# MLP up products on TensorE: moving columns read, and PSUM columns written, in another order

## The chip, the cores and the metric

The kernel runs on one core of a Trainium2 chip. A core has TensorE (PE in the profile; PEld is its weight load), VectorE (DVE), ScalarE (ACT), GpSimd (POOL) and SyncE (SP, which here mostly issues transfers). The metric is the device time of one execution in microseconds (us); lower is better.

## The reference

A two-layer decoder trunk on 1024 positions of width 1024, all in float32. Layer 0 mixes tokens by a gated DeltaNet, layer 1 by sliding-window attention. The part that matters here is the gated MLP, which each layer has once:

```python
D_FF = 2816

def causal_dwconv(x, w):
    k_w = w.shape[0]
    t = x.shape[1]
    xp = jnp.pad(x, ((0, 0), (k_w - 1, 0), (0, 0)))
    y = w[0] * xp[:, 0:t]
    for i in range(1, k_w):
        y = y + w[i] * xp[:, i:i + t]
    return y

def conv_ffn(x, w_up, conv_w, w_down):
    u = causal_dwconv(x @ w_up, conv_w)
    gate, val = u[..., :D_FF], u[..., D_FF:]
    return (jax.nn.silu(gate) * val) @ w_down

def reference(...):
    h = x
    for i in range(DEPTH):
        ...
        h = h + conv_ffn(rmsnorm(h, norm_ffn[i]), f_w_up[i], f_conv[i], f_w_down[i])
        ...
    return rmsnorm(h, norm_final)
```

The change touches how `x @ w_up` is computed, and not what it gives.

## The kernel before

Activations lie transposed: 128 channels on the partitions, 1024 positions along the free dimension, eight such tiles for the width of 1024. A matmul takes a 128 x 128 block of weights as its stationary operand and streams 512 columns (positions) of activations through it into one PSUM bank of 512 columns. To keep float32 accuracy with the faster float32r type, each operand is split into a high and a low part, and a product is made of three passes: high by high, high weights by low activations, low weights by high activations.

The MLP is the function `ffn`. For each of 22 values of j (`NF`) it computes a 128-row tile of the gate and one of the value. The two tiles, the two halves of the positions and the even and odd input tiles make a 2 x 2 by 2 x 2 block product, and it is done with seven products instead of eight (Winograd's form of Strassen's scheme). `Mix.add` makes the seven activation operands: `b11`, `b21`, `b22` are plain blocks, `t1` to `t4` are sums and differences of blocks. In the profile `b11` is in the tile named b (high part in columns 0 to 511, low part in 512 to 1023), `t1` and `t2` share the tiles t12h and t12l (one half each), `t3` and `t4` share t34h and t34l, and `b21` and `b22` share x1h and x1l. `weights` loads and adds up the weight blocks and splits them into `whi` and `wlo`.

`prod` runs one product: over four input tiles k, three matmuls each, so 12 matmuls into one PSUM bank. `up` runs the seven for one j, in the order b11, t2, t3, t1, b21, t4, b22. p1 takes b11 and later b21, p7 takes t3 and later t4, p5 takes t1 and later b22, p6 takes t2 alone. p6 is in the pool whose banks the profile names d, the others in the one named mm. Between them VectorE and ScalarE take the sums out of PSUM, and `step` runs pieces of the down product (gh and gl by dhi and dlo in the profile), 12 matmuls each, into banks named d.

What sets the order: SyncE, VectorE, ScalarE, GpSimd and TensorE each run their own queue in the order in which the program was written, as far as the tile framework keeps it. `E.pinned = True` keeps TensorE's matmuls in program order through `ffn`'s loop. All matmuls are issued from one helper, so the profile puts them on line 152, and groups are told apart by their tiles.

The prediction also uses rows from elsewhere: line 654, GpSimd's triangular solve in layer 0, where the pass j works on rows of j + 1 elements in a 16 x 16 table (15 - j rows of them, 16 apart); line 736, where ScalarE copies four blocks of 64 columns out of PSUM to places 128 apart; and lines 778 and 1347, ScalarE's copies out of PSUM without a break.

Of the kernel before, what the change touches and what calls it, by code (L numbers as in the profile page):

```python
# [90 lines left out]

def ch(t, c):
    return t[:, c * P:(c + 1) * P]


def hs(h):
# [12 lines left out]
def kernel(  # L109
# [104 lines left out]
    def passes(ps, wh, wl, xs, h, k0=0):  # L214

        n = len(xs)
        for k, (xh, xl) in enumerate(xs):
            w_h, w_l = ch(wh, k0 + k), ch(wl, k0 + k)
            E.matmul(ps, w_h, xh[:, hs(h)], start=k == 0, stop=False)
            yield  # L220
            E.matmul(ps, w_h, xl[:, hs(h)], start=False, stop=False)
            yield
            E.matmul(ps, w_l, xh[:, hs(h)], start=False, stop=k == n - 1)
            yield

    def mm3(ps, wh, wl, xs, h, k0=0, first=True, last=True):
        n = len(xs)
        for k, (xh, xl) in enumerate(xs):
            w_h, w_l = ch(wh, k0 + k), ch(wl, k0 + k)
            E.matmul(ps, w_h, xh[:, hs(h)], start=first and k == 0, stop=False)  # L230
            E.matmul(ps, w_h, xl[:, hs(h)], start=False, stop=False)
            E.matmul(ps, w_l, xh[:, hs(h)], start=False, stop=last and k == n - 1)
# [26 lines left out]
    class Norm:  # L259
# [23 lines left out]
        def factor(self):  # L283
            ps = pst()
            for c in range(NCH):
                E.matmul(ps[:, c:c + 1], ch(self.sq, c), ones[:, 0:1], start=True, stop=True)
            S.put(self.sq)
            ms = sm.tile([P, NCH], F32, tag="ms", name="ms")
            V.tensor_scalar(ms, ps[:, 0:NCH], 1.0 / D, EPS, MUL, ADD)
            r = sm.tile([P, NCH], F32, tag="r", name="r")  # L290
            G.tensor_tensor(r, ms, mhalf, ALU.pow)
            self.r = r
# [916 lines left out]
    def ffn(l, mix, nxt):  # L1209
# [60 lines left out]

        def prod(ps, w, xn, ks=range(KT // 2), first=True):
            wh, wl = w
            for k in ks:
                xh, xl = mix.x[xn][k]
                mm = dict(skip_group_check=not first)
                E.matmul(ps, ch(wh, k), xh, start=first and k == 0, stop=False, **mm)
                E.matmul(ps, ch(wh, k), xl, start=False, stop=False, **mm)
                E.matmul(ps, ch(wl, k), xh, start=False, stop=k == KT // 2 - 1, **mm)
# [52 lines left out]
        def up(j, early, late):  # L1331
# [12 lines left out]
            else:  # L1344
                p1 = pmt()
                prod(p1, *take(), "b11")
                A.copy(dd, p1)
                for _ in range(early[0]):
                    step()
                p6 = pdt()  # L1350
                prod(p6, *take(), "t2")
                V.tensor_tensor(dd, p6, dd, SUB)
                if j == 1:
# [8 lines left out]
                gated(j - 1)  # L1362
                p7 = pmt()
                prod(p7, *take(), "t3")
                V.tensor_tensor(zh(z2, 1), p7, dd, ADD)  # L1365
                p5 = pmt()
# [81 lines left out]
        for j in range(NF):  # L1448
            n = len(todo) + len(loaded)
# [234 lines left out]
```

## Time and profile before

| | |
|---|---|
| median of 2 runs | 2771.84 us |
| lowest and highest run | 2769.29 and 2774.39 us |
| profiled execution, its own time | 2775.09 us |
| its span, first to last instruction | 2773.3 us |
| mean granted TensorE clock | 0.985 |
| MLP up products, layer 0 | 742 to 1398 us of the span |
| MLP up products, layer 1 | 1930 to 2588 us of the span |
| HBM traffic | 232.56 MB read, 99.68 MB written |

The page of the profile comes from one execution. Busy time of an engine is the union of its instructions, so overlapping matmuls count once. In a row of a group, the number after the x is the count, then come the busy time in us and the mean duration in ns of one, then the idle time of the engine just before them. In a row of the timeline the two numbers ahead are start and duration in us.

### The profile page before, as it was taken

Reading aid. Unit: us, or ns where it says so; the run is one execution under the profiler, and the core shown is the slowest. Engines: PE = TensorE matmul, PEld = TensorE weight load, DVE = VectorE, ACT = ScalarE, POOL = GpSimd, SP = SyncE. Lnnn points to the kernel's source line nnn. Section 1 sums busy time; section 2 is a strip of 40 time slices with the busy share of each in tenths; the row PEclk is TensorE's granted clock in tenths of the full one; section 3 lists DMA queues with packets and bytes.
Section 4 is the critical chain, followed back from the end, with each engine's and each line's share of the span. In section 5 each row is a group of like instructions: output and inputs, shape, how many; then the busy total and the mean of one; then the engine's idle time right before and its main releaser. Section 6 shows DMA issues by size and latency. Waiting matters only on the chain. (4 is left out here: it accounts for less than half of the span.)

```text
span 2773.3 us, 35355 instructions
## 1 busy us (share of the span) xinstructions
PE 2664.3 (96%) x12914; PEld 2141.2 (77%) x12914; DVE 1790.9 (65%) x2579; ACT 1119.6 (40%) x2184; POOL 1175.5 (42%) x1104
## 2 busy tenths in 40 slices
PE   9899999999899999999999999999999999999998
PEld 7778878878677787787777776667777888888786
DVE  6555555564787777677764336656867767677745
ACT  5443334442633333333343235555433333333443
POOL 5444444342454444445432323334544444444354
PEclk9999999999999999999999999999999999999999
DMA  5222221232225555555432221222255555554323
GB/s 175 88 72 57 64 59 55 64 101 70 103 87 184 184 175 196 197 192 182 162 106 72 82 69 46 56 68 100 86 173 181 185 188 176 201 196 154 108 91 109
DMA packets 167069, 340.83 MB, mean 123 GB/s; under 512 B 38896, under 2 KB 91504, under 8 KB 166896
## 3 DMA queue, kind: packets, MB, share of 16 engines
q1 hardware_dynamic: 166032, 337.20, 36.9%
q8 instruction: 101, 1.65, 0.3%
q10 hardware_dynamic: 864, 1.38, 0.1%
q14 instruction: 72, 0.59, 0.1%
HBM read 232.56 MB, written 99.68 MB: 120 GB/s over the span
## 5 line engine op out<-in xcount | busy, mean ns | idle before, releaser
L201 POOL TENSOR_TENSOR wlo<-wraw,whi 128x512 fp32r<-128x512 f32 (+1 forms) x204 | 273.6, 1358 | 407.4 <-ACT whi L198 365.0
L152 PE MATMUL mm<-xh,whi 128*128 128x512 f32 x856 | 358.2, 418 | 3.6 <-ACT xh L254 2.7
L152 PE MATMUL mm<-xh,wlo 128*128 128x512 f32 x856 | 349.7, 409 | 0.0
L152 PE MATMUL mm<-xl,whi 128*128 128x512 f32 x856 | 347.1, 406 | 0.5 <-DVE xl L255 0.5
L211 POOL TENSOR_TENSOR dlo<-draw,dhi 128x256 fp32r<-128x256 f32 (+1 forms) x160 | 164.9, 1031 | 350.5 <-ACT dhi L210 329.2
L1226 POOL TENSOR_TENSOR wlo<-wraw,whi 128x512 fp32r<-128x512 f32 x132 | 188.9, 1439 | 155.4 <-ACT whi L1225 155.4
L1226 POOL TENSOR_TENSOR wlo<-sa,whi 128x512 fp32r<-128x512 f32 x132 | 194.1, 1471 | 139.2 <-ACT whi L1225 139.2
L152 PE MATMUL d<-gh,dhi 128*128 128x512 f32 x576 | 229.7, 399 | 6.4 <-DVE h L1325 6.0
L152 PE MATMUL d<-gh,dlo 128*128 128x512 f32 x576 | 228.3, 396 | 0.0
L152 PE MATMUL d<-gl,dhi 128*128 128x512 f32 x576 | 228.2, 396 | 0.0
L1325 DVE TENSOR_TENSOR h<-h,d 128x512 f32<-128x512 f32 x288 | 193.8, 682 | 32.9 <-PE d L152 32.4
L198 ACT CAST whi<-wraw 128x1024 fp32r<-128x1024 f32 (+3 forms) x122 | 100.1, 822 | 234.2 <-PE mm L152 114.2
L152 PEld LDWEIGHTS mm<-xh,wlo 128*128 128x128 f32 x856 | 163.4, 191 | 34.0
L152 PEld LDWEIGHTS mm<-xh,whi 128*128 128x128 f32 x856 | 163.9, 191 | 31.1 <-ACT xh L254 3.1
L152 PEld LDWEIGHTS mm<-xl,whi 128*128 128x128 f32 x856 | 164.3, 192 | 27.5 <-DVE xl L255 1.3
L152 PE MATMUL mm<-t34h,whi 128*128 128x512 f32 x352 | 141.4, 402 | 5.8 <-DVE zv L1365 4.7
L321 DVE SCALAR_TENSOR_TENSOR yf<-zg,fcv,yf 128x1024 f32<-128x1024 f32 x88 | 131.0, 1489 | 18.3 <-ACT yf L319 16.7
L152 PE MATMUL mm<-t34l,whi 128*128 128x512 f32 x352 | 140.9, 400 | 0.8 <-POOL t34l L914 0.8
L152 PE MATMUL mm<-t34h,wlo 128*128 128x512 f32 x352 | 140.7, 400 | 0.0
L152 PE MATMUL mm<-x1l,whi 128*128 128x512 f32 x352 | 139.4, 396 | 0.2
L152 PE MATMUL mm<-x1h,whi 128*128 128x512 f32 x352 | 139.4, 396 | 0.0
L152 PE MATMUL mm<-x1h,wlo 128*128 128x512 f32 x352 | 139.2, 396 | 0.0
(376 smaller groups left out, 6559.6 us busy)
## 6 DMA issues: line engine op xcount, KB each, us to landing
hf<-h SPq DMA_DIRECT2D x160, 512.0 KB, 3.3
h<-hf SPq DMA_DIRECT2D x160, 512.0 KB, 4.2
wraw<-f_up SPq DMA_DIRECT2D x88, 512.0 KB, 3.4
draw<-f_down SPq DMA_DIRECT2D x144, 128.0 KB, 2.3
wraw<-a_in SPq DMA_DIRECT2D x32, 512.0 KB, 3.6
wraw<-g_w SPq DMA_DIRECT2D x24, 512.0 KB, 3.3
row<-rowd SPq DMA_DIRECT2D x16, 512.0 KB, 3.9
wraw<-b_in SPq DMA_DIRECT2D x12, 512.0 KB, 3.6
```

The lines of the kernel that those rows point to most:

```text
L152: i = nc.tensor.matmul(*a, **k)
L198: A.copy(hi, raw)
L201: G.tensor_tensor(lo[:, i:j], raw[:, i:j], hi[:, i:j].bitcast(F32), SUB)
L211: G.tensor_tensor(lo, raw, hi[:, :].bitcast(F32), SUB)
L321: V.scalar_tensor_tensor(dst[:, a:b], z[:, a + i:b + i], w[:, i:i + 1], dst[:, a:b], MUL, ADD)
L1226: G.tensor_tensor(lo, src, hi.bitcast(F32), SUB)
L1325: V.tensor_tensor(t[:, hs(h)], t[:, hs(h)], ps, ADD)
```

## The change

`prod` passes its PSUM bank and its moving operands through a function of the product's name before the matmuls are issued. The function views columns 0 to 511 as m parts of equal length and takes n columns from each part in turn. With `runs(2, 2)`, t2 reads columns 0, 1, then 256, 257, then 2, 3, then 258, 259, and so on, and writes its results to the same columns of the bank. So each result lands where it did before; only the order in time within a matmul differs. The stationary operands keep theirs. With `runs(256, 2)` the order is that of before, and `b11` passes through as it is.

```diff
+def runs(n, m):
+
+    return lambda ap: ap[:, 0:512].rearrange("p (m r n) -> p r m n", m=m, n=n)
+
+
+ORDERS = {
+    "b11": lambda ap: ap,
+    "t2": runs(2, 2),
+    "t3": runs(8, 2),
+    "t1": runs(16, 2),
+    "b21": runs(32, 2),
+    "t4": runs(16, 4),
+    "b22": runs(256, 2),
+}
...
         def prod(ps, w, xn, ks=range(KT // 2), first=True):
             wh, wl = w
+            order = ORDERS[xn]
+            ps = order(ps)
             for k in ks:
-                xh, xl = mix.x[xn][k]
+                xh, xl = (order(v) for v in mix.x[xn][k])
                 mm = dict(skip_group_check=not first)
                 E.matmul(ps, ch(wh, k), xh, start=first and k == 0, stop=False, **mm)
```

Every engine has the same instructions in the same order, with the same waits. On TensorE the shape of five products' matmuls differs (partitions first, then the sizes of the nested loops over the columns); the helper's line moves from 152 to 168. TensorE before, at the end of t2 and the start of the down product's matmuls, at one j in layer 0:

```order
L152 MATMUL d_10987<-t12h_225_6195,whi_10819 128x512
L152 MATMUL d_10987<-t12l_226_6196,whi_10819 128x512
L152 MATMUL d_10987<-t12h_225_6195,wlo_10820 128x512
L152 MATMUL d_10987<-t12h_235_6298,whi_10819 128x512
L152 MATMUL d_10987<-t12l_236_6299,whi_10819 128x512
L152 MATMUL d_10987<-t12h_235_6298,wlo_10820 128x512
L152 MATMUL d_11003<-gh_369_10309,dhi_10964 128x512
```

TensorE after the change, at the same place:

```order
L168 MATMUL d_10987<-t12h_225_6195,whi_10819 128x128x2x2
L168 MATMUL d_10987<-t12l_226_6196,whi_10819 128x128x2x2
L168 MATMUL d_10987<-t12h_225_6195,wlo_10820 128x128x2x2
L168 MATMUL d_10987<-t12h_235_6298,whi_10819 128x128x2x2
L168 MATMUL d_10987<-t12l_236_6299,whi_10819 128x128x2x2
L168 MATMUL d_10987<-t12h_235_6298,wlo_10820 128x128x2x2
L168 MATMUL d_11003<-gh_369_10309,dhi_10964 128x512
```

The rows stand where they stood; t2's 512 columns are now 128 rounds of two parts with two columns each, and the down product's matmul is unchanged.

TensorE before, at the same j, from the end of t1 to the start of b21:

```order
L152 MATMUL mm_11051<-t12h_235_6298,whi_10856 128x512
L152 MATMUL mm_11051<-t12l_236_6299,whi_10856 128x512
L152 MATMUL mm_11051<-t12h_235_6298,wlo_10857 128x512
L152 MATMUL mm_10944<-x1h_207_6051,whi_10945 128x512
L152 MATMUL mm_10944<-x1l_208_6052,whi_10945 128x512
L152 MATMUL mm_10944<-x1h_207_6051,wlo_10946 128x512
```

TensorE after the change, at the same place:

```order
L168 MATMUL mm_11051<-t12h_235_6298,whi_10856 128x16x2x16
L168 MATMUL mm_11051<-t12l_236_6299,whi_10856 128x16x2x16
L168 MATMUL mm_11051<-t12h_235_6298,wlo_10857 128x16x2x16
L168 MATMUL mm_10944<-x1h_207_6051,whi_10945 128x8x2x32
L168 MATMUL mm_10944<-x1l_208_6052,whi_10945 128x8x2x32
L168 MATMUL mm_10944<-x1h_207_6051,wlo_10946 128x8x2x32
```

Nothing moved here either; t1 has 16 rounds of two parts with 16 columns each, b21 has 8 rounds of two parts with 32 columns each.

## The prediction

> **What bounds the kernel now.** I read the page first: its line of busy times and, among the forty slices, the row of the granted TensorE clock.
>
> ```profile
> span 2773.3 us, 35355 instructions
> PE 2664.3 (96%) x12914; PEld 2141.2 (77%) x12914; DVE 1790.9 (65%) x2579; ACT 1119.6 (40%) x2184; POOL 1175.5 (42%) x1104
> PEclk9999999999999999999999999999999999999999
> ```
>
> TensorE (PE) is busy for 96% of the span, with the clock nearly always open, and the next engine, VectorE (DVE), for 65%. Since 96% is an average, I then asked for the two stretches that hold the MLP up products, one per layer (columns: length, busy time of each engine, granted clock, DMA share, GB/s):
>
> ```profile
> core 0: us, PE busy (x) PEld busy (x) DVE busy (x) ACT busy (x) POOL busy (x), PEclk, DMA share, GB/s
> 742.00:1398.00 656.00, 649.60 (x2775) 519.20 (x2774) 483.92 (x575) 243.40 (x378) 306.15 (x231) 1.00 0.51 174
> 1930.00:2588.00 658.00, 649.75 (x2772) 519.65 (x2771) 481.30 (x574) 243.53 (x376) 298.00 (x228) 0.99 0.50 170
> ```
>
> PE stands idle for 656.00 - 649.60 = 6.4 us in the first and 658.00 - 649.75 = 8.25 us in the second. What it waits for in the second is listed by the view of waits (total us, times, longest):
>
> ```profile
> PE d L152 <- DVE h L1325: 4.1, 3, 1.8
> PE mm L152 <- DVE zv L1365: 2.3, 1, 2.3
> PE mm L152 <- DVE t12l L914: 0.7, 1, 0.7
> ```
>
> So no engine covers PE there. Time added to the up products' matmuls comes out at the end nearly one for one: at most 6.4 + 8.25 = 14.65 us of idle time could swallow some. Time taken off them would be gained until VectorE, at 483.92 of 656 us, is the bound, which is far away.
>
> A matmul's own duration (396 ns and more in the groups below) overlaps its neighbours; what counts is the step from one start to the next. It is read from the timeline of PE, here at one value of j where the products stand in a row; each of these rows is the first of a product's twelve matmuls (start us, duration us):
>
> ```profile
> 1017.82 0.40 PE L152 MATMUL d<-t12h,whi 128*128 128x512 f32 x1
> ...
> 1020.62 0.40 PE L152 MATMUL d<-gh,dhi 128*128 128x512 f32 x1
> ...
> 1023.45 0.40 PE L152 MATMUL mm<-t34h,whi 128*128 128x512 f32 x1
> ...
> 1026.25 0.40 PE L152 MATMUL mm<-t12h,whi 128*128 128x512 f32 x1
> ...
> 1029.05 0.40 PE L152 MATMUL mm<-x1h,whi 128*128 128x512 f32 x1
> ...
> 1031.85 0.40 PE L152 MATMUL mm<-t34h,whi 128*128 128x512 f32 x1
> ...
> 1034.65 0.40 PE L152 MATMUL d<-gh,dhi 128*128 128x512 f32 x1
> ```
>
> t2 runs from 1017.82 to 1020.62, then t3, t1, b21 and t4 each start 2.80 us after the one before, and t4 ends at 1034.65. Each of the five takes 2.80 us, that is 2.80 / 12 = 0.2333 us a matmul, whichever tile it reads and whichever PSUM bank it writes.
>
> **The change, part by part.** It adds and removes no instruction on any engine and moves none; every wait stays on the instruction that had it. What differs is the order in which a matmul walks its 512 moving columns, and with them its 512 PSUM columns. How many matmuls that touches follows from the groups (the page's, all of one form; count after the x):
>
> ```profile
> L152 PE MATMUL mm<-t34h,whi 128*128 128x512 f32 x352 | 141.4, 402 | 5.8 <-DVE zv L1365 4.7 <-DVE zv L1342 1.2
> L152 PE MATMUL mm<-x1h,whi 128*128 128x512 f32 x352 | 139.4, 396 | 0.0
> L152 PE MATMUL mm<-b,whi 128*128 128x512 f32 x352 | 110.8, 396 | 0.0
> L152 PE MATMUL d<-t12h,whi 128*128 128x512 f32 x176 | 69.6, 396 | 0.0
> L152 PE MATMUL mm<-t12h,whi 128*128 128x512 f32 x176 | 69.6, 396 | 0.0
> ```
>
> Each tile pair has three such groups (high by high, low by high, high by low). t34 serves t3 and t4: 3 x 352 = 1056, so 528 each. t12 serves t2 (into d) and t1 (into mm): 3 x 176 = 528 each. x1 serves b21 and b22, 528 each. b11 keeps its order by the table, and b22's two runs of 256, one behind the other, are again columns 0 to 511 in order. So the last two are unchanged, and five products, 5 x 528 = 2640 matmuls, walk in pieces. In one matmul of t2 there are 512 / 2 = 256 pieces, of t3 64, of t1 32, of b21 16 and of t4 32, together 400.
>
> The sum is 2640 matmuls times an unknown extra per matmul. No matmul of this kernel walks in pieces, so the extra is bounded by the nearest rows. The first is what the stream of columns is limited by now. In layer 1 there is a stretch in which the granted clock is half (window row, then timeline):
>
> ```profile
> 2025.80:2029.20 3.40, 3.40 (x10) 2.62 (x9) 1.79 (x3) 0.44 (x2) 1.03 (x1) 0.50 0.38 154
> ```
>
> ```profile
> 2027.83 0.63 PE L152 MATMUL mm<-t34h,whi 128*128 128x512 f32 x1
> 2028.26 0.63 PE L152 MATMUL mm<-t34l,whi 128*128 128x512 f32 x1
> 2028.69 0.63 PE L152 MATMUL mm<-t34h,wlo 128*128 128x512 f32 x1
> ```
>
> There the step is (2028.69 - 2027.83) / 2 = 0.43 us. Half of it is 0.215, and at the full clock the step is 0.2333: about 0.018 us of each step isn't the array's clock. Matmuls of 256 columns show the same pace, from 1663.91 to 1664.38 in four steps, 0.1175 each, or 0.46 ns a column, like 0.2333 / 512:
>
> ```profile
> 1663.91 0.28 PE L152 MATMUL d<-kh,qa 128*128 128x256 f32 x1
> ...
> 1664.38 0.40 PE L152 MATMUL mm<-xh,whi 128*128 128x512 f32 x1
> ```
>
> So something that goes with the columns, perhaps the way they are read or written, is slightly slower than the array. That is why I don't call a cost impossible. From below, 0.215 us is the pace of the array: the change can gain at most 0.018 x 2640 = 48 us. From above, the one slower pace in these rows is 0.43: 0.197 x 2640 = 520 us.
>
> The second set of rows is how other engines fare with broken patterns. POOL's line 654 works on a 16 x 16 table, at 544.42 (its second pass) on 14 rows of 2 and at 481.46 (its last but one) on 2 rows of 14, both 28 elements, and both reading and writing the table in place. ACT's line 736 writes 256 elements as four runs of 64, and 128 and 512 elements without a break stand beside it:
>
> ```profile
> 544.42 0.24 POOL L654 TENSOR_TENSOR sys<-sys 64x28 f32<-64x28 f32 x1
> ```
>
> ```profile
> 481.46 0.23 POOL L654 TENSOR_TENSOR sys<-sys 64x28 f32<-64x28 f32 x1
> ```
>
> ```profile
> L778 ACT COPY u<-s 128x128 f32<-128x128 f32 x64 | 16.9, 264 | 55.8 <-PE s L152 55.5
> L1347 ACT COPY sb<-mm 128x512 f32<-128x512 f32 x42 | 24.4, 582 | 46.5 <-PE mm L152 46.5
> L736 ACT COPY X<-d 64x256 f32<-64x256 f32 x16 | 5.9, 367 | 31.8 <-PE d L156 31.8
> ```
>
> On POOL twelve more pieces, each of two 4-byte elements as in t2, cost 0.01 us or nothing (the rows are rounded to that). On ACT the straight line between 264 and 582 ns gives 264 + 128 x 318 / 384 = 370 ns for 256 elements, and the broken write took 367. An access pattern with pieces is free there. I take the extra as 0 for all five products, since these are the only rows of broken patterns and the shortest piece among them is also two elements; both ends stay for the range.
>
> [...]
>
> Against the profiled execution, 2775.09 us (a span of 2773.3 and 1.79 around it), the sum is 2775.09 + 0. That execution stands 3.25 us above the median of the two runs, 2771.84, so I forecast 2772.
>
> **The rivals.**
>
> First, a fixed toll at each new piece. At one column's time, 0.2333 / 512 = 0.456 ns, the five products pay 528 x 400 x 0.456 ns = 96 us: 2868, slower by 3.5%. It decides (2% is 55.4 us, about what a measurement of this kernel can tell from no change) from 55.4 us / 211200 pieces = 0.26 ns a piece. For it: POOL's 0.01 us over twelve pieces would be 0.8 ns. Against it: ACT's row, and that rounding can make all of POOL's difference.
>
> Second, only the shortest pieces pay. If operands or results are moved in groups wider than two columns, t2 needs a group for each pair, its matmuls take twice as long, and nothing else changes: 528 x 0.2333 = 123 us, 2895, slower by 4.4%. For it: the pace of 0.2333 against the array's 0.215 says that moving columns is near its limit already, with no slack for twice as many groups. Against it: no row shows the width of a group.
>
> Third, a gain. If the stream's excess came from columns that follow each other too closely, spreading them could bring the array's pace: 48 us, 2724, faster by 1.7% and so within 2%. Nothing in the rows shows such a conflict.
>
> Fourth, every broken matmul falls to a slower pace. With the half-clock row's 0.43 us: 520 us, 3292, slower by 18.8%. For it: there is no matmul here to show that it isn't so. Against it: the rows of ACT and POOL, with runs of 64 and of 2.
>
> That the change does nothing at all is true of two of the seven products (b11 and b22); for the other five the instructions carry the new pattern, so it isn't a rival for the whole.
>
> **How the numbers follow.** No cost 0.70, since the nearest rows show none; a toll per piece 0.10; t2 alone 0.12, because the stream seems near a limit; every broken matmul slow 0.05; a gain 0.02; anything else 0.01, put with faster. The forecast is the likeliest, 2772. Its own range is 2760 to 2785: the runs shown and the profiled one lie between 2769.29 and 2775.09, and up to 10 us more is left for a few ns on each of 2640 matmuls (4 ns is 10.6 us). With the first rival that makes 0.80, but not all of the 0.70 lies in its own range, so the range takes in the second too: 2760 to 2900. The fourth is left out. Faster by over 2%: 0.01. Within 2%: 0.70 + 0.02 = 0.72. Slower: 0.10 + 0.12 + 0.05 = 0.27.
>
> **What would show it.** In the new timeline t2, t3, t1, b21 and t4 should each still take 2.80 us from first start to next product's start. A toll per piece shows as t2 at 2.80 + 12 x 256 x 0.456 ns = 4.20 us, with t3 at 3.15, t1 and t4 at 2.98 and b21 at 2.89: excess in proportion to the pieces. The second rival shows t2 at 5.60 and the rest at 2.80. The fourth shows all five at about 5.2. b11 and b22 stay at 2.80 in every case; if they don't, something else than the order of columns has changed. PE's idle time in the two stretches should stay at 6.4 and 8.25 us. The forecast is wrong if any of the five products takes 3.0 us or more.

## The result and the profile after

The changed kernel takes 2809.17 us (median of two runs, 2807.48 and 2810.86) against 2771.84 before: a ratio of 1.0131, 95% interval 1.0100 to 1.0161. That is 37 us more, within 2% and clear of noise. The profiled execution took 2810.86 us with a span of 2809.1.

The view from which the prediction took the time of each product, the timeline of PE at one j in layer 0, now shows where the time goes (first matmul of each product; start us, duration us):

```profile
1012.14 0.63 PE L168 MATMUL mm<-b,whi 128*128 128x512 f32 x2
...
1014.94 0.40 PE L168 MATMUL d<-gh,dhi 128*128 128x512 f32 x1
...
1017.74 0.49 PE L168 MATMUL d<-t12h,whi 128*128 128x512 f32 x1
...
1021.73 0.40 PE L168 MATMUL d<-gh,dhi 128*128 128x512 f32 x1
...
1024.53 0.41 PE L168 MATMUL mm<-t34h,whi 128*128 128x512 f32 x1
...
1027.44 0.40 PE L168 MATMUL mm<-t12h,whi 128*128 128x512 f32 x1
...
1030.32 0.40 PE L168 MATMUL mm<-x1h,whi 128*128 128x512 f32 x1
...
1033.12 0.40 PE L168 MATMUL mm<-t34h,whi 128*128 128x512 f32 x1
...
1035.93 0.40 PE L168 MATMUL d<-gh,dhi 128*128 128x512 f32 x1
```

b11 takes 1014.94 - 1012.14 = 2.80 us as before. t2 takes 1021.73 - 1017.74 = 3.99, that is 3.99 / 12 = 0.3325 us a matmul in place of 0.2333. t3 takes 2.91, t1 2.88, b21 2.80 and t4 2.81. Over all j of both layers the medians are the same to 0.01 us. With 44 products of each kind (22 values of j in two layers) the extra is 44 x (1.19 + 0.11 + 0.08 + 0.01) = 61 us, of which t2 has 52. The time rose by 37. The rest is found in the windows after the change, to be held against the prediction's (length, busy times, granted clock, DMA share, GB/s):

```profile
736.00:1413.00 677.00, 674.78 (x2771) 521.89 (x2770) 486.33 (x574) 246.33 (x378) 302.09 (x231) 1.00 0.50 168
1947.00:2624.00 677.00, 674.78 (x2770) 521.84 (x2770) 483.69 (x574) 245.56 (x376) 293.55 (x228) 1.00 0.48 165
```

The MLP stretches grew from 656 and 658 us to 677 each, by 40 together. PE's idle time in them fell from 6.4 and 8.25 us to 677.00 - 674.78 = 2.22 each: 10 us of the added time went into waits that PE had anyway. The view of waits after, for layer 1, shows what is left:

```profile
PE mm L168 <- DVE zv L1383: 1.3, 1, 1.3
PE mm L168 <- DVE t12l L930: 0.7, 1, 0.7
PE mm L168 <- POOL t34l L930: 0.3, 1, 0.3
```

The 4.1 us for `h` of the down product are gone; that VectorE now has more time between two products would explain it. Two more things went with the waits. After three of the four longest waits before the change the clock was halved for a while, and the step from matmul to matmul was 0.43 us (granted clock 0.50 in the prediction's row from 2025.80 to 2029.20): the trace has about 25 such steps in the two stretches before and 3 after, which is 4 us. And a wait cost more than its idle time, as these rows of before show (in brackets the idle time ahead of a matmul and what ended it):

```profile
2023.20 0.40 PE L152 MATMUL d<-gh,dlo 128*128 128x512 f32 x1
2025.41 0.50 PE L152 MATMUL d<-gh,dhi 128*128 128x512 f32 x1 [1.81 <-DVE h L1325]
2025.74 0.59 PE L152 MATMUL d<-gl,dhi 128*128 128x512 f32 x1
```

Across 1.81 us of idle time the step from start to start is 2.21, and the next is 0.33, in place of 0.2333 each: 0.27 us beside the idle time. The trace has 20 waits in the two stretches before and 6 after, and 14 x 0.27 is another 4 us, an estimate from this one wait. 61 - 10 - 4 - 4 is 43, against 40 by the windows, whose ends are rounded; from the first matmul on b to the last on x1 of each layer the trace gives 42.

The stretch ahead of the MLP in layer 0, which the change does not touch, lasts 736 us in place of 743 up to that first matmul on b. That is not the change's doing: it lasts 734 in the experiment below that puts t2 back in order, and 743 again in the one that keeps the reading orders alone, whose whole time is 2814.84.

### The profile page after: what moved, and what is told of

Its sections match the earlier page's. It is cut to its first block, busy times and chain, and to the rows that moved or that the text cites. A ratio compares the mean times of both kernels' runs of the same rounds, so it can differ in the third digit from the quotient of the medians.

```text
span 2809.1 us, 35384 instructions
## 1 busy us (share of the span) xinstructions
PE 2713.3 (97%) x12914; PEld 2145.1 (76%) x12914; DVE 1794.9 (64%) x2579; ACT 1125.1 (40%) x2184; POOL 1166.7 (42%) x1104
## 5 line engine op out<-in xcount | busy, mean ns | idle before, releaser
L1242 POOL TENSOR_TENSOR wlo<-sa,whi 128x512 fp32r<-128x512 f32 x132 | 184.8, 1400 | 188.9 <-ACT whi L1241 182.0
L226 ACT CAST dhi<-draw 128x256 fp32r<-128x256 f32 (+1 forms) x160 | 66.5, 416 | 203.7 <-PE d L168 149.4
```

What stands on the lines that cost most here:

```text
L226: A.copy(hi, raw)
L1242: G.tensor_tensor(lo, src, hi.bitcast(F32), SUB)
```

## The experiments

All the runs below state the time of one kernel beside runs of the kernel before on the same chip. Where a product's time is given, it is worked out as above, from its first matmul's start to that of what follows it, at one j in layer 0. Where no number of runs is given, the time is that of a single execution; the runs of the kernel before lie between 2764.83 and 2781.29 us, so single times tell little of differences below 17 us, and those runs are read by the times of their products.

**t2 back in order.** Is it t2 that carries the loss?

```diff
-    "t2": runs(2, 2),
+    "t2": lambda ap: ap,
```

> The kernel after the change, with t2 back to columns 0 to 511 in order; t3, t1, b21 and t4 keep their pieces. In the changed kernel's timeline t2 takes 3.99 us a product in place of 2.80 and t3 and t1 about 0.1 us more than 2.80. Theory: t2 carries the loss, so this kernel stands at the time before plus what t3 and t1 cost, 44 products each: 44 x (0.11 + 0.08) = 8 us, about 2780 (ratio 1.003). Rival: the loss is spread, or comes from waits that the new orders cause elsewhere; then it stays near 2800 (ratio 1.010).

2781.92 us (ten runs) against 2773.43: a ratio of 1.0029, 95% interval 1.0020 to 1.0039. The forecast of 1.003 holds: t3 and t1 cost 8.5 us in time, close to the 8 us that their matmuls add, and t2 carries the rest.

**t2 alone.** The counterpart: only t2 in pieces.

```diff
-    "t3": runs(8, 2),
-    "t1": runs(16, 2),
-    "b21": runs(32, 2),
-    "t4": runs(16, 4),
-    "b22": runs(256, 2),
+    "t3": lambda ap: ap,
+    "t1": lambda ap: ap,
+    "b21": lambda ap: ap,
+    "t4": lambda ap: ap,
+    "b22": lambda ap: ap,
```

> Only t2 is read and written in pieces of two from two parts, the other six in order. In the matmuls t2 costs 44 x 1.19 = 52 us. Theory swallowed (part of it goes into TensorE's waits for VectorE in the MLP stages and the half-clock stretches that follow them, as in the changed kernel): about 2809 - 8.5 = 2800, ratio 1.010. Rival (it comes out whole): 2773 + 52 = 2825, ratio 1.019.

2805.39 us (four runs) against 2778.06, a ratio of 1.0104, 95% interval 1.0077 to 1.0131: as "swallowed" had it, and below the rival's 1.019. Its windows show the same shrinking of idle time, 674.00 - 671.30 = 2.7 us in layer 0:

```profile
738.00:1412.00 674.00, 671.30 (x2770) 520.24 (x2769) 484.36 (x574) 244.79 (x378) 304.92 (x231) 1.00 0.49 168
```

**Reading in pieces, writing in order.** The prediction could not tell reading from writing.

```diff
-            ps = order(ps)
```

> The moving columns are read in the new orders but the PSUM columns are written 0 to 511 in order, so the columns of five products come out permuted: what is computed for a position is another one's. Theory R (the cost lies in reading SBUF in pieces): t2 stays at 3.99 us, t3 at 2.91, t1 at 2.88, the time at about 2809. Theory W (it lies in writing PSUM in pieces): all seven at 2.80 and the time at about 2772. Both sides together needed: in between, t2 between 2.80 and 3.99.

2814.84 us. The timeline of this kernel, t2 and t3 and what follows:

```profile
1024.37 0.49 PE L168 MATMUL d<-t12h,whi 128*128 128x512 f32 x1
...
1028.36 0.40 PE L168 MATMUL d<-gh,dhi 128*128 128x512 f32 x1
...
1031.16 0.41 PE L168 MATMUL mm<-t34h,whi 128*128 128x512 f32 x1
...
1034.07 0.40 PE L168 MATMUL mm<-t12h,whi 128*128 128x512 f32 x1
...
1036.95 0.40 PE L168 MATMUL mm<-x1h,whi 128*128 128x512 f32 x1
```

t2 takes 3.99 us, t3 2.91, t1 2.88: what they take in the changed kernel, to the last digit.

**Writing in pieces, reading in order.**

```diff
-                xh, xl = (order(v) for v in mix.x[xn][k])
+                xh, xl = mix.x[xn][k]
```

> The moving columns are read 0 to 511 in order and the PSUM columns are written in the new orders, so again columns of five products are permuted. Theory R: all seven at 2.80 us, the time at about 2772. Theory W: t2 at 3.99, t3 at 2.91, t1 at 2.88, the time at about 2809.

2773.13 us, no longer than before (2773.43). t2 in its timeline:

```profile
1015.12 0.40 PE L168 MATMUL d<-t12h,whi 128*128 128x512 f32 x1
...
1017.92 0.40 PE L168 MATMUL d<-gh,dhi 128*128 128x512 f32 x1
```

2.80 us, and t3 and t1 take 2.80 in this trace too. So the whole cost of the change lies in reading the moving columns out of SBUF (t2 takes 3.99 us where the reading alone is in pieces, 2.80 where the writing alone is); writing PSUM columns in the change's orders, pieces of two to 32, is free. No run wrote pieces of one column.

**The same orders in other products.** Does the loss belong to the order, or to t2's tile?

```diff
+    "t2": runs(32, 2),
+    "t3": runs(2, 2),
+    "t1": runs(16, 4),
+    "b21": runs(16, 2),
+    "t4": runs(8, 2),
+    "b22": runs(64, 2),
```

> The orders of the change given to other products: pieces of 2 from two parts to t3, 8 from two to t4, 16 from two to b21, 16 from four to t1, 32 from two to t2, 64 from two to b22, b11 in order. Theory order (the loss belongs to the order of reading): t3 takes 3.99 us, t4 2.91, b21 2.88, t1 2.81, t2, b22 and b11 2.80. Rival place (it belongs to the operand's tile or bank): t2 stays slow, t1 and t3 stay 0.1 us above 2.80 and t4 and b21 at 2.80. Time about 2809 by the first.

2819.25 us, against a forecast of about 2809. t3, now in pieces of two, takes 1031.08 - 1027.08 = 4.00 us, and t4 and b21 have taken over the tenth of a microsecond:

```profile
1027.08 0.49 PE L168 MATMUL mm<-t34h,whi 128*128 128x512 f32 x1
...
1031.08 0.41 PE L168 MATMUL mm<-t12h,whi 128*128 128x512 f32 x1
...
1033.90 0.40 PE L168 MATMUL mm<-x1h,whi 128*128 128x512 f32 x1
...
1036.78 0.41 PE L168 MATMUL mm<-t34h,whi 128*128 128x512 f32 x1
...
1039.69 0.40 PE L168 MATMUL d<-gh,dhi 128*128 128x512 f32 x1
```

t1 (16 from four parts) takes 2.82, b21 (16 from two) 2.88, t4 (8 from two) 2.91. The loss goes with the order.

**Pieces of two from more parts.** A toll for each piece, or for the distance to the next?

```diff
+    "b11": runs(2, 4),
+    "t2": runs(2, 2),
+    "t3": runs(2, 8),
+    "t1": runs(2, 16),
+    "b21": runs(2, 32),
+    "t4": runs(2, 64),
+    "b22": runs(2, 128),
```

> All seven products in pieces of two columns, 256 pieces each, from a different number of parts, so that one piece lies 256 columns from the next in t2 (2 parts), 128 in b11 (4), 64 in t3 (8), 32 in t1 (16), 16 in b21 (32), 8 in t4 (64) and 4 in b22 (128). Theory count (a toll per piece): every product takes about 3.99 us, and the MLP stages together are about 44 x 6 x 1.19 = 314 us longer than in the changed kernel, about 3120. Theory distance (the toll depends on how far the next piece lies): t2 at 3.99 as before, and the others fall towards 2.80 as the parts draw near; half of them free gives about 2960.

3509.75 us: both theories failed, for every other order was far dearer than t2's. The rows are those of b11, then of t2 and what follows:

```profile
1014.68 1.13 PE L168 MATMUL mm<-b,whi 128*128 128x512 f32 x2
...
1020.10 0.41 PE L168 MATMUL d<-gh,dhi 128*128 128x512 f32 x1
...
1022.91 0.49 PE L168 MATMUL d<-t12h,whi 128*128 128x512 f32 x1
...
1026.93 0.40 PE L168 MATMUL d<-gh,dhi 128*128 128x512 f32 x1
...
1029.74 0.71 PE L168 MATMUL mm<-t34h,whi 128*128 128x512 f32 x1
...
1035.71 0.64 PE L168 MATMUL mm<-t12h,whi 128*128 128x512 f32 x1
...
1041.20 0.62 PE L168 MATMUL mm<-x1h,whi 128*128 128x512 f32 x1
...
1046.40 0.64 PE L168 MATMUL mm<-t34h,whi 128*128 128x512 f32 x1
...
1051.91 0.41 PE L168 MATMUL d<-gh,dhi 128*128 128x512 f32 x1
```

t2 takes 4.02 us, b11 (4 parts) 5.42, t3 (8) 5.97, t1 (16) 5.49, b21 (32) 5.20, t4 (64) 5.51. From four parts on, that is about double the 2.80 of reading in order. A new theory, an estimate from these times, came from it: the time of a matmul goes with the groups of four neighbouring columns that its pieces touch. In order, 512 columns are 128 groups, 0.2333 us / 128 = 1.82 ns a group. A piece of two touches a group and uses half of it: 256 groups, 5.2 to 6.0 us / 12 / 256 = 1.7 to 1.9 ns a group. Then t2 is the exception, at 4.02 us / 12 / 256 = 1.31 ns a group. In its order, with two parts alone, a group comes up again after one other piece; no run shows whether that is why. Nor does any trace show a fetch: that columns are fetched in such groups, as the expectations below put it, is the author's reading of the times. This run also writes PSUM in these orders, and writing pieces of two from more than two parts was never run alone; that it is free there too is not shown.

**Pieces of four.** If the time goes with the groups of four that are touched, these cost no more than reading in order.

```diff
+    "b11": runs(4, 2),
+    "t2": runs(4, 4),
+    "t3": runs(4, 8),
+    "t1": runs(4, 16),
+    "b21": runs(4, 32),
+    "t4": runs(4, 64),
+    "b22": lambda ap: ap,
```

> Pieces of four columns, 128 a matmul, in six products from 2 (t2), 4 (t3's neighbour order: b11 has 2, t2 has 4), so: b11 2 parts, t2 4, t3 8, t1 16, b21 32, t4 64; b22 in order. Theory group (moving columns are fetched in groups of four neighbours, about 1.82 ns a group: 128 groups give the 233 ns of a matmul in order, 256 groups of which half is thrown away the 433 to 496 ns that pieces of two from 4 to 128 parts took): pieces of four waste nothing, so all seven products take 2.80 us (b11, with two parts, at most 0.1 more) and the time is about 2772. Rival toll (a price per piece, 0.8 to 1.0 ns by the pieces of two): 128 pieces add 100 to 130 ns a matmul, t2, t3, t1, b21 and t4 take 4.0 to 4.4 us, and the time is about 3080.

2808.99 us, neither of the two times.

```profile
1024.24 0.44 PE L168 MATMUL mm<-t34h,whi 128*128 128x512 f32 x1
...
1027.57 0.41 PE L168 MATMUL mm<-t12h,whi 128*128 128x512 f32 x1
...
1030.53 0.40 PE L168 MATMUL mm<-x1h,whi 128*128 128x512 f32 x1
...
1033.31 0.39 PE L168 MATMUL mm<-t34h,whi 128*128 128x512 f32 x1
...
1036.11 0.40 PE L168 MATMUL d<-gh,dhi 128*128 128x512 f32 x1
```

t4, 128 pieces that lie 8 columns apart, takes 2.80 us, and b21, 16 apart, 2.78: no toll per piece at all. But t1 (32 apart) takes 2.96 and t3 (64 apart) 3.33, and in the same trace t2 (128 apart) takes 3.19 and b11 (256 apart) 3.04. So "group" missed four of its seven products, and there is a second, smaller effect beside the groups: pieces of four that lie 32 or more columns apart cost more, though not in proportion to the distance.

**Longer pieces.**

```diff
+    "b11": runs(8, 2),
+    "t2": runs(8, 4),
+    "t3": runs(8, 8),
+    "t1": runs(16, 8),
+    "b21": runs(16, 16),
+    "t4": runs(8, 32),
+    "b22": runs(32, 4),
```

> Pieces of 8 from two parts in b11, from four in t2, from eight in t3, from 32 in t4, of 16 from eight in t1 and from sixteen in b21, of 32 from four in b22. Theory group: no group of four is cut, so t2, t3, t4, t1, b21 and b22 take 2.80 to 2.82 us; b11, two parts 256 columns apart, takes 2.91 as t3 did in the change. Rival toll: at 0.8 to 1.0 ns a piece, the three with 64 pieces take 3.4 to 3.6 us, those with 32 take 3.1 to 3.2, b22 with 16 takes 2.95 to 3.0. A gain anywhere (under 2.75 us) would speak for neighbours that get in each other's way when read in order.

2781.26 us. b11 took 2.91 us as forecast and t4 and b22 2.80, but t1 took 2.86 and b21 2.88, t2 was faster than in order, 2.76, and t3 took 2.97: the forecast of 2.80 to 2.82 holds for two of six. The single matmuls of t3 differ:

```profile
1052.32 0.39 PE L168 MATMUL mm<-t34h,whi 128*128 128x512 f32 x1
1052.55 0.38 PE L168 MATMUL mm<-t34l,whi 128*128 128x512 f32 x1
1052.77 0.43 PE L168 MATMUL mm<-t34h,wlo 128*128 128x512 f32 x1
1053.03 0.41 PE L168 MATMUL mm<-t34h,whi 128*128 128x512 f32 x1
```

The steps are 0.23, 0.22 and 0.26 us, in the same order. The first and the third read the same columns of the same tile and differ in their weights (`whi` and `wlo`), so the operand's place in SBUF alone does not settle the second effect. What does stays open.

**Shifted by two columns.** The test that tells "group" from "length": the same pieces, once starting at a multiple of four and once two columns later. For t1, t3 and b21 `Mix.add` keeps a second view of the operand, which `prod` takes.

```diff
+                self.off["t3"].append([t[:, 2:514] for t in t34s])
...
-                xh, xl = (order(v) for v in mix.x[xn][k])
+                xh, xl = (order(v) for v in mix.off.get(xn, mix.x[xn])[k])
...
+    "t2": runs(4, 64),
+    "t3": runs(4, 64),
+    "t1": lambda ap: ap,
+    "b21": runs(8, 32),
+    "t4": runs(8, 32),
```

> The same lengths of piece, aligned and shifted. t2 and t4 read pieces of 4 from 64 parts and of 8 from 32 parts from column 0 of their operand, t3 and b21 the same two orders from column 2, t1 in order from column 2; b11 and b22 are as before. The shifted products take 512 columns that start two later, so their last two columns come from the other half of the tile and what they give belongs to other positions. Theory group (four neighbours that start at a multiple of four are fetched together): t2 and t4 2.80 us; t3's pieces each touch two groups, 256 in all, 5.2 to 5.5 us as pieces of two took; b21's pieces of 8 touch three, 192 in all, 192 x 1.75 = 336 ns, 4.0 us; t1 touches 129, 2.80 to 2.85. Time about 2772 + 44 x (2.6 + 1.2) = 2930 and less. Rival length (only the length of a piece counts, wherever it starts): all seven at 2.75 to 2.85 us, time about 2772.

2923.64 us.

```profile
1040.74 0.40 PE L168 MATMUL d<-t12h,whi 128*128 128x512 f32 x1
...
1043.53 0.39 PE L168 MATMUL d<-gh,dhi 128*128 128x512 f32 x1
...
1046.38 0.62 PE L168 MATMUL mm<-t34h,whi 128*128 128x512 f32 x1
...
1051.81 0.41 PE L168 MATMUL mm<-t12h,whi 128*128 128x512 f32 x1
...
1054.64 0.49 PE L168 MATMUL mm<-x1h,whi 128*128 128x512 f32 x1
...
1058.68 0.41 PE L168 MATMUL mm<-t34h,whi 128*128 128x512 f32 x1
...
1061.47 0.39 PE L168 MATMUL d<-gh,dhi 128*128 128x512 f32 x1
```

Pieces of four take 2.79 us from column 0 (t2) and 5.43 from column 2 (t3); both write PSUM in the same order, so the difference lies in the reading. Pieces of eight take 2.79 (t4) and 4.04 (b21). In order the shift costs next to nothing (t1, 2.83). All as "group" forecast, b21's 4.0 too: 192 groups at 1.75 ns. Each piece of t3 touches two groups, two columns of each, so 256 groups: 5.43 us / 12 / 256 = 1.77 ns a group.

**Two kernels with the order that was faster.** First all seven up products in pieces of 8 from four parts, then also the projections, down products and gates (`mm3` and `passes`).

```diff
+    "b11": runs(8, 4),
...
+    "b22": runs(8, 4),
```

> All seven products in pieces of 8 from four parts, the one order that was faster than reading in order (t2 took 229.9 ns a matmul in place of 233.3). Theory order (the gain goes with the order): 3696 matmuls x 3.4 ns = 12.6 us, about 2760, ratio 0.995. Rival place (it depends on where operand and order meet in memory, as the 222 to 270 ns of t3 with eight parts suggest): some products gain, some lose, within 8 us of the time before.

2765.26 us (ten runs) against 2771.34, a ratio of 0.9976, 95% interval 0.9964 to 0.9988. Each product got faster, to medians of 2.76 to 2.78 us over all j, so "place" falls. t3 takes 2.76 here:

```profile
1043.47 0.40 PE L168 MATMUL mm<-t34h,whi 128*128 128x512 f32 x1
...
1046.23 0.40 PE L168 MATMUL mm<-t12h,whi 128*128 128x512 f32 x1
```

But the time fell by 6 us and not by 12.6. PE's idle time in layer 0's MLP is now 660.00 - 645.90 = 14.1 us, where it was 6.4, and the waits are mostly for the `h` of the down product again, 9.2 us (in layer 1 it is 6.99, where it was 8.25):

```profile
734.00:1394.00 660.00, 645.90 (x2773) 518.97 (x2772) 482.30 (x574) 242.77 (x378) 307.40 (x231) 0.99 0.49 172
```

```profile
PE d L168 <- DVE h L1343: 9.2, 7, 1.8
```

```diff
+ORDER = runs(8, 4)
...
+            po, xh, xl = (ORDER(v) for v in (ps, xh[:, hs(h)], xl[:, hs(h)]))
-            E.matmul(ps, w_h, xh[:, hs(h)], start=first and k == 0, stop=False)
+            E.matmul(po, w_h, xh, start=first and k == 0, stop=False)
...
```

> Pieces of 8 from four parts in the up products and in nearly all other matmuls of 512 columns (projections, down products, gates), about 9600 in all. Theory order: 9600 x 3.4 ns = 33 us off, about 2740, ratio 0.988. Rival place: gains and losses cancel, ratio between 0.995 and 1.01.

2755.05 us (seven runs) against 2771.34, a ratio of 0.9943, 95% interval 0.9923 to 0.9964: half of the forecast gain. The matmuls did get faster, those of the down product from a median step of 234 ns to 231. But PE's idle time in the two MLP stretches is now 17.22 and 11.76 us, 14 more than before, with 12.6 us of waits for `h` in layer 0 alone. It is the fastest of all these kernels.

```profile
PE d L171 <- DVE h L1348: 12.6, 11, 1.8
```

## Why the prediction was right, and where it was not

The time lies within the range of 2760 to 2900 and within 2%. That it is within 2% is luck: the 0.72 stood for no cost and a gain, and what came was a slower t2. The 61 us that the matmuls gained in length, all on top of 2771.84, would have made 2833, slower by 2.2%; it was the waits giving way that kept the time below. The range holds 2809 since it was stretched to take in the second rival. The forecast of 2772, by its own last sentence, was wrong: t2 took 3.99 us, over the 3.0 that was set.

What bounds the kernel was right in the main. PE has no cover in these stretches: with t2's pieces taken away the time was 2781.92, what t3 and t1 add to the matmuls and no less. Two sentences on it were not right. Idle time was to swallow at most 14.65 us; 10 us of it went (it fell to 2.22 us in each stretch, where the prediction had it stay at 6.4 and 8.25), but with the half-clock steps and the rest of each wait some 18 us were swallowed. The sums of the rivals left all this out, and it is the second-largest term of this case. And time taken off was to be gained until VectorE is the bound, "which is far away"; in the kernel with pieces of eight, 12.6 us taken off gave 6, while PE's idle time in the two stretches rose from 14.65 to 21.09 us.

The counts were right: b11 and b22 stayed at 2.80 us, and the other five carried the pattern.

The step that failed is "I take the extra as 0 for all five products, since these are the only rows of broken patterns". Pieces that cost nothing on POOL (0.24 us against 0.23) and ACT (367 ns against 370) did cost time where TensorE reads. For t4 and b21 zero was right (0.01 us a product and less), for t3 and t1 nearly so (0.11 and 0.08), and for t2 it missed 1.19 us a product, 52 us in all. The better row stood beside it: the step of 0.2333 us at the full clock against 0.215, half of the step at half the clock, from which the prediction itself took it that something that goes with the columns is slower than the array. The second rival was built on this row, and its pattern came nearest: t2 pays most by far. Its price of 123 us for t2 was more than twice too high, against 52; t2 reads from two parts only, and from four and more parts the doubling is there, 5.2 to 6.0 us a product. Its premise, that operands are moved in groups wider than two columns, was an estimate, and no trace shows the moving itself. What the runs show are times that go with groups of four columns that start at multiples of four: 2.79 us a product for pieces of four from column 0, 5.43 from column 2.

The first rival, a toll per piece, falls: 128 pieces of four, 8 columns apart, cost nothing (2.80 us a product), while by a toll per piece they would cost half as much as 256. The fourth, every broken matmul slow, falls with t4 and b21, at 2.81 and 2.80 us. The third, a gain, did not show in this change; with another order it exists, at 0.23 us in place of 0.2333, far from the 0.215 that the prediction worked out from the half-clock rows as the array's pace. Whether a cost would lie in reading or in writing, which the prediction left open, is settled for the change's orders: writing in these pieces is free (t2, t3 and t1 at 2.80 us). And a measurement of this kernel can tell far less than 2%: ten runs told the 8.5 us of t3 and t1 from nothing.

Open are why pieces of two from two parts (3.99 to 4.02 us a product) are cheaper than from four and more (5.20 to 5.97), and what makes the second effect.

## What to carry to other kernels

Judge a moving operand's access pattern by how many aligned groups of four float32 columns each matmul touches, not by whether it is contiguous: in these runs pieces of a multiple of four that start at a multiple of four cost between nothing and 0.53 us on the 2.80 of a product, and pieces of two, or pieces of four and eight that start two columns off, cost 1.2 to 3.2 us. Writing PSUM in the change's pieces cost nothing (2.80 us a product). And where PE is at 99% of a stretch, a loss or a gain still doesn't come out whole: 61 us of added matmul time made the two stretches some 40 us longer, and 12.6 us of saved time gave 6, since waits for VectorE shrink and grow against it.

## What was not expected of the hardware

Reading in order isn't the fastest: pieces of eight from four parts took 2.76 to 2.78 us a product against 2.80, in all seven products; why is not known. With eight parts single matmuls of t3 went down to 0.22 us, but others of the same product took 0.26. And a group of four columns took about as long when half of it was wasted (1.7 to 1.9 ns, but for the 1.3 of pieces of two from two parts) as when all of it was used in order (1.82 ns): from four parts on, a wasted half was paid in full.
